# Weight parts side by side in one tile, and the feed-forward pool 32 bytes lower, in a float32 decoder trunk on one Trainium2 core

## Chip, core and metric

The kernel runs on one NeuronCore of a Trainium2 chip. The metric is the device time of one execution in microseconds (us). SBUF is the on-chip memory of 128 partitions from which every operand of the matrix engine is read; a tile's address is a byte offset that is the same in all its partitions.

## What is computed

Two layers on 512 tokens of width 1024, float32. Each layer is a half-step SwiGLU feed-forward block, a mixer, and a second half-step feed-forward block; the mixer is causal pooling in layer 0 and multi-head latent attention (MLA) in layer 1.

```python
def swiglu(h, w_gate, w_up, w_down):
    return (jax.nn.silu(h @ w_gate) * (h @ w_up)) @ w_down

for i in range(DEPTH):
    h = rmsnorm(x, ffn1_norm[i])
    x = x + FFN_HALF * swiglu(h, ffn1_w_gate[i], ffn1_w_up[i], ffn1_w_down[i])
    h = rmsnorm(x, mix_norm[i])
    x = x + (pool_mixer(h, ...) if i % 2 == 0 else mla_mixer(h, ...))
    h = rmsnorm(x, ffn2_norm[i])
    x = x + FFN_HALF * swiglu(h, ffn2_w_gate[i], ffn2_w_up[i], ffn2_w_down[i])
```

The widths are 1024 for the model and 2816 (22 blocks of 128) for the feed-forward layer.

## The kernel before

**Split products.** Every float32 operand is split into a high part and a low part (`split`, L113 to L122): ScalarE (ACT) writes the high part, VectorE (DVE) the difference. A product is then three matmuls per block of 128 rows (`mm3`, L107): high weights by high data, high weights by low data, low weights by high data. The weights are the stationary operand, which is loaded before each matmul (row kind PEld, LDWEIGHTS); the data are the moving operand, 256 or 512 columns of a `slot` tile.

**Weights.** SyncE's queue loads each block of 128 by 1024 weights into a tile `raw`, and `split` turns it into `whi` and `wlo`. The pool `wp` has three buffers each of `raw`, `whi` and `wlo`. `weights` (L124) makes a `whi` or `wlo` tile of 32 float32 more than is needed, so that `off` can start the data 64 bytes into it: `load_w` (L129) uses offset 0 in the feed-forward and most MLA products, 64 in `latent` (L702). The three buffers of a tag are taken in turn.

**A feed-forward block** works through the 22 blocks of its hidden width in chunks of 4, 6, 6, 6. The first chunk uses plain products of 512 columns. In the other three, `Two` (L367) computes two hidden blocks by two halves of the model width and two halves of the tokens with seven products instead of eight: each product is 4 row blocks of 3 matmuls with 256 columns. `w_sums` (L336) prepares its weights. Four of the seven products have their weights in `whi`/`wlo` at offset 64: a11, a12 from `raw`, and s1, s2 from a sum tile `s`. Three (s3, s4 and a22) have them in tiles `hi`/`lo` of the pool `fp`, which lives as long as the feed-forward block. Six `Two` make one chunk, 504 matmuls; there are 12 such chunks and so 72 `Two`. After each chunk the down projection makes 8 tiles of weights by `load_w` at offset 0, with 3 matmuls of 512 columns for each hidden block of the chunk, 18 in the later chunks, and adds the result to the stream `xs`.

**Pools.** SBUF pools lie behind one another in the order `cp`, `xp`, `sp` (45 `slot` tiles), `wp`, `kp`, `tp`, and then, one at a time, `fp` (feed-forward), `rp` (tables), `pp` (pooling) or `mp` (MLA). The order of the instructions on an engine follows the code, up to small shifts that a scheduler makes.

**The shared rotary key** of MLA (L726) takes a `whi` tile alone, without a `wlo`, and puts both parts into it. From then on `whi` is one buffer ahead of `wlo` in its turn.

Of the kernel before, what the change touches and what calls it, by code (L numbers as in the profile page):

```python
# [10 lines left out]
F32R = mybir.dt.float32r  # L11
# [6 lines left out]
P = 128  # L18
# [4 lines left out]
NT = S // P  # L23
# [8 lines left out]
WC = 1024  # L32
# [44 lines left out]
def trunk(ctx: ExitStack, tc: tile.TileContext, a: dict, out: bass.AP):  # L77
# [5 lines left out]
    wp = ctx.enter_context(tc.tile_pool(name="wp", bufs=3))  # L83
# [8 lines left out]
    def aux():  # L92
        return pb.tile([P, S], F32, tag="aux", name="aux")
# [7 lines left out]
    def small(n, dt=F32, tag=None, bufs=3):  # L101
        return tp.tile([P, n], dt, tag=tag or f"sm{n}", name="small", bufs=bufs)

    def mm(ps, lhsT, rhs, start, stop, skip=False):
        nc.tensor.matmul(ps, lhsT, rhs, start=start, stop=stop, skip_group_check=skip)  # L105
# [7 lines left out]
    def split(src, hi, lo, scale=None):  # L113

        if scale is None:
            nc.scalar.activation(hi, src, AF.Copy)  # L116
            nc.vector.tensor_tensor(out=lo, in0=src, in1=hi.bitcast(F32), op=ALU.subtract)  # L117
        else:
            nc.scalar.activation(hi, src, AF.Copy, scale=scale)  # L119
            nc.vector.scalar_tensor_tensor(  # L120
                out=lo, in0=src, scalar=scale, in1=hi.bitcast(F32), op0=ALU.mult, op1=ALU.subtract
            )  # L122

    def weights(tag, off=0):  # L124

        t = wp.tile([P, WC + 32], F32R, tag=tag, name=tag)
        return t[:, off // 4 : off // 4 + WC]

    def load_w(src, cols, off=0):  # L129
        raw = wp.tile([P, WC], F32, tag="raw", name="raw")  # L130
        hi, lo = weights("whi", off), weights("wlo", off)
        nc.sync.dma_start(raw[:, :cols], src)
        split(raw[:, :cols], hi[:, :cols], lo[:, :cols])
        return hi, lo
# [12 lines left out]
    def rsqrt(v, n, out=None):  # L147
        i = small(n, I32, tag=f"rsi{n}")
        nc.vector.tensor_scalar(i, v.bitcast(I32), 1, None, op0=ALU.logical_shift_right)
        y = small(n, tag=f"rsy{n}")  # L150
        nc.vector.tensor_scalar(
            y.bitcast(I32), i, -1.0, float(0x5F3759DF), op0=ALU.mult, op1=ALU.add
        )
        for last in (False, False, True):
            t = small(n, tag=f"rst{n}")
            nc.vector.tensor_mul(t, y, y)
            nc.vector.scalar_tensor_tensor(
                out=t, in0=t, scalar=-0.5, in1=v, op0=ALU.mult, op1=ALU.mult
            )
            y2 = out if last and out is not None else small(n, tag=f"rsy{n}")  # L160
            nc.vector.scalar_tensor_tensor(
                out=y2, in0=t, scalar=1.5, in1=y, op0=ALU.add, op1=ALU.mult
            )
            y = y2
        return y


    class Prep:
# [31 lines left out]
        def rstd(self):  # L200

            ps = aux()
            for i in range(NT):
                mm(ps[:, i : i + 1], self.sq[:, i * P : (i + 1) * P], ones[:, 0:1], True, True)
            v = small(NT, tag="ms")
            nc.vector.tensor_scalar(v, ps[:, :NT], 1.0 / D, EPS, op0=ALU.mult, op1=ALU.add)
            return rsqrt(v, NT, tp.tile([P, NT], F32, tag="rstd", name="rstd", bufs=2))

# [11 lines left out]
    def opening(wg, wu, prep):  # L220

        half = WC // 2
        ws = []
        for _ in range(2):
            raw = wp.tile([P, WC], F32, tag="raw", name="raw")
            ws.append((raw, weights("whi"), weights("wlo")))

        def load_half(e):
            for w, (raw, _, _) in zip((wg, wu), ws):
                nc.sync.dma_start(  # L230
                    raw[:, e * half : (e + 1) * half], w[:, e * half : (e + 1) * half]
                )

        def split_half(e):
            hs = slice(e * half, (e + 1) * half)
            for raw, hi, lo in ws:
                split(raw[:, hs], hi[:, hs], lo[:, hs])

        def load_x(j):
            nc.sync.dma_start(xs[j], a["xT"][j])  # L240

        load_x(0)
        load_half(0)
        for j in range(1, 4):
            load_x(j)
        load_half(1)
        for j in range(4, KD):
            load_x(j)
        nc.sync.dma_start(ident, a["ident"])
        ps = [acc(), acc()]  # L250
        for k in range(KD):
            prep.halve(k)
            if k % 4 == 0:
                split_half(k // 4)
            ks = slice(k * P, (k + 1) * P)
            for p, (_, hi, lo) in zip(ps, ws):
                mm3(p, (hi[:, ks], lo[:, ks]), prep.halves[k], k == 0, k == KD - 1)
        for k in (*range(1, KD), 0):
            prep.square(k)
        return ps  # L260
# [6 lines left out]
    def ffn_in(fp, wg, wu, wd, prep, nxt, first, final):  # L267
# [68 lines left out]
        def w_sums(top, low):  # L336

            hw = WC // 2
            rt = wp.tile([P, WC], F32, tag="raw", name="raw")
            rl = wp.tile([P, WC], F32, tag="raw", name="raw")  # L340
            nc.sync.dma_start(rt, top)
            nc.sync.dma_start(rl, low)
            a11, a12, a21, a22 = rt[:, :hw], rt[:, hw:], rl[:, :hw], rl[:, hw:]
            s12 = fp.tile([P, WC], F32, tag="s", name="s", bufs=2)
            s34 = fp.tile([P, WC], F32, tag="s", name="s", bufs=2)
            s1, s2, s3, s4 = s12[:, :hw], s12[:, hw:], s34[:, :hw], s34[:, hw:]
            for out, x, y, op in (
                (s1, a21, a22, ALU.add), (s2, s1, a11, ALU.subtract),
                (s3, a11, a21, ALU.subtract), (s4, a12, s2, ALU.subtract),
            ):  # L350
                nc.vector.tensor_tensor(out=out, in0=x, in1=y, op=op)  # L351

            def halves(src, n, tag):
                if tag == "w":
                    hi, lo = weights("whi", 64), weights("wlo", 64)
                else:
                    hi, lo = (
                        fp.tile([P, n], F32R, tag=tag + e, name=e, bufs=2) for e in ("hi", "lo")
                    )
                split(src, hi, lo)  # L360
                return [(hi[:, c : c + hw], lo[:, c : c + hw]) for c in range(0, n, hw)]

            a11, a12 = halves(rt, WC, "w")
            s3, s4 = halves(s34, WC, "c")
            s1, s2 = halves(s12, WC, "w")
            (a22,) = halves(a22, hw, "d")
            return a11, a12, a22, s1, s2, s3, s4  # L367
# [90 lines left out]
        for f0, f1 in CHUNKS:  # L458
# [38 lines left out]
            for m in range(KD):  # L497
                if f0 == 0 and m % 2 and m > 1:
                    x_sums(m // 2)
                hi, lo = load_w(wd[m][:, f0 * P : f1 * P], nf * P)  # L500
# [183 lines left out]
    def mla_layer(prep, nxt):  # L684
        with tc.tile_pool(name="mp", bufs=1) as mp:
# [16 lines left out]

            def latent(m):

                hi, lo = load_w(a["w_in"][m], WC, 64)
                p = acc()
                for k in range(KD):
                    ks = slice(k * P, (k + 1) * P)
                    mm3(p, (hi[:, ks], lo[:, ks]), xh[k], k == 0, k == KD - 1)
                lat[m] = (slot(), slot())  # L710
                split(p, *lat[m], gains[:, G_Q + m : G_Q + m + 1])
                e = m // KQ
                if e not in sums:
                    sums[e] = kp.tile([P, S], F32, tag="rows", name="lsq", bufs=2)
                    nc.scalar.activation(sums[e], p, AF.Square)
                else:
                    q = work()
                    nc.scalar.activation(q, p, AF.Square)
                    nc.vector.tensor_add(sums[e], sums[e], q)
# [4 lines left out]


            raw = wp.tile([P, WC], F32, tag="raw", name="raw")  # L726
            both = weights("whi")
            nc.sync.dma_start(raw[:, : KD * DR], a["w_kpe"])
            wv = both.rearrange("p (k e f) -> p k e f", k=KD, e=2)
            split(  # L730
# [49 lines left out]
            def latent_rms(e, n):  # L780

                ps = aux()
                for i in range(NT):
                    mm(ps[:, i : i + 1], sums[e][:, i * P : (i + 1) * P], ones[:, 0:1], True, True)
                v = small(NT, tag="ms")
                nc.vector.scalar_tensor_tensor(
                    out=v, in0=ps[:, :NT], scalar=1.0 / n, in1=r2, op0=ALU.mult, op1=ALU.mult
                )
                nc.vector.tensor_scalar(v, v, EPS, None, op0=ALU.add)
                f, f2 = keep(NT, f"f{e}"), keep(NT, f"ff{e}")  # L790
                nc.vector.tensor_mul(f, rsqrt(v, NT), r)
                nc.vector.tensor_mul(f2, f, f)
                return f, f2
# [389 lines left out]
```

## Time and profile before

| what | value |
|---|---|
| median of 3 runs | 1646.99 us (1646.85 to 1647.1) |
| the profiled execution's own time | 1648.0 us |
| its span in the trace | 1646.2 us |
| PE (matmul) busy | 1635.4 us, 99% of the span |
| PEld (weight loads) busy | 1476.7 us, 90% |
| DVE busy | 1250.8 us, 76% |
| ACT busy | 823.7 us, 50% |
| POOL (GpSimd) busy | 47.1 us, 3% |
| DMA | 161.74 MB, mean 98 GB/s |

Matmuls are pipelined: a row's duration reaches from a matmul's start to its modelled end, and the next has long begun by then. What a matmul costs in a dense stretch is therefore the distance between two starts, which the view of instructions in order of time gives, and not the mean duration of a group.

### The profile page before, as it was taken

The numbers are of one execution on the slowest core, as the hardware profiler recorded it, in microseconds if no ns is written. First come the engines' busy times: TensorE is split into PE (matmuls) and PEld (weight loads), VectorE is DVE, ScalarE is ACT, GpSimd is POOL, SyncE is SP. The second block draws the span as 40 slices with busy tenths as digits, with TensorE's granted clock in tenths as the row PEclk, the third lists the DMA queues.
The fourth block names the chain that finished last, engine by engine and source line by source line (L and its number), as shares of the span: only waits on it lengthen the run. The fifth ranks groups of instructions, "written<-read, shape, count | busy, mean of one in ns | idle before, by whom it ended". The sixth has DMA issues, their size and how long they took to land.

```text
span 1646.2 us, 26418 instructions
## 1 busy us (share of the span) xinstructions
PE 1635.4 (99%) x10502; PEld 1476.7 (90%) x10502; DVE 1250.8 (76%) x2114; ACT 823.7 (50%) x1409; POOL 47.1 (3%) x133
## 2 busy tenths in 40 slices
PE   8999999999999999999999999999999999999999
PEld 6898999988898989988999989888898889999897
DVE  8985858799986758669858667647788899677673
ACT  6453535554553535434635445447675455445351
POOL 0000000000000000000000000002321000000000
PEclk9999999999999999999999999999999999999999
DMA  5333324231333233332323243322122224333432
GB/s 169 103 111 114 107 82 127 84 114 58 119 107 110 93 106 103 96 103 84 125 85 124 81 125 93 95 93 62 46 59 77 73 62 136 90 116 97 118 94 90
DMA packets 52827, 161.74 MB, mean 98 GB/s; under 512 B 6240, under 2 KB 7008, under 8 KB 52704
## 3 DMA queue, kind: packets, MB, share of 16 engines
q1 hardware_dynamic: 52128, 159.34, 31.7%
q8 instruction: 82, 1.34, 0.3%
q10 hardware_dynamic: 576, 0.72, 0.1%
q14 instruction: 41, 0.34, 0.1%
HBM read 157.94 MB, written 2.10 MB: 97 GB/s over the span
## 4 chain that ended last, share of the span: by engine, by line
PE 96%; DVE 2%; ACT 1%; DMA 1%; issue 0%; SPq 0%; POOL 0%; DVEq 0%; POOLq 0%
PE acc L105 94%; PE aux L697 1%; PE aux L105 1%; PE aux L978 0%; DVE wlo L117 0%; DMA raw<-in_ffn_up 0%; DMA raw<-in_ffn_gate 0%; DVE s L351 0%; DVE slot L117 0%; ACT slot L119 0%; DVE x L510 0%; ACT whi L116 0%; ACT work L184 0%; DVE sqacc L185 0%; ACT work L959 0%
## 5 line engine op out<-in xcount | busy, mean ns | idle before, releaser
L105 PE MATMUL acc<-slot,whi 128*128 128x256 f32 (+1 forms) x4508 | 1091.2, 334 | 5.5 <-ACT whi L116 5.1
L105 PEld LDWEIGHTS acc<-slot,whi 128*128 128x128 f32 x4508 | 763.1, 189 | 102.2 <-ACT whi L116 5.1
L105 PE MATMUL acc<-slot,wlo 128*128 128x512 f32 (+1 forms) x2246 | 751.3, 335 | 0.2 <-DVE wlo L117 0.2
L105 PEld LDWEIGHTS acc<-slot,wlo 128*128 128x128 f32 x2246 | 422.2, 188 | 45.2 <-DVE wlo L117 0.9
L116 ACT ACTIVATE whi<-raw 128x1024 fp32r<-128x1024 f32 (+2 forms) x269 | 246.0, 915 | 378.9 <-PE acc L105 262.5
L117 DVE TENSOR_TENSOR wlo<-raw,whi 128x1024 fp32r<-128x1024 f32 (+2 forms) x268 | 278.9, 1042 | 105.1 <-ACT whi L116 103.5
L105 PE MATMUL acc<-slot,hi 128*128 128x256 f32 x1728 | 308.8, 279 | 0.0
L105 PEld LDWEIGHTS acc<-slot,hi 128*128 128x128 f32 x1728 | 263.3, 188 | 0.0
L105 PE MATMUL acc<-slot,lo 128*128 128x256 f32 x864 | 240.7, 279 | 0.0
L510 DVE SCALAR_TENSOR_TENSOR x<-acc,x 128x512 f32<-128x512 f32 x129 | 88.2, 684 | 134.5 <-PE acc L105 134.4
L105 PEld LDWEIGHTS acc<-slot,lo 128*128 128x128 f32 x864 | 162.4, 188 | 0.0
L398 ACT ACTIVATE m<-acc 128x256 f32<-128x256 f32 x216 | 81.9, 380 | 96.5 <-PE acc L105 95.9
L117 DVE TENSOR_TENSOR lo<-s,hi 128x1024 fp32r<-128x1024 f32 x72 | 88.0, 1222 | 55.1 <-ACT hi L116 53.5
L351 DVE TENSOR_TENSOR s<-raw 128x512 f32<-128x512 f32 x144 | 96.1, 685 | 19.3 <-DMA raw<-in_ffn_up 14.9
L116 ACT ACTIVATE hi<-s 128x1024 fp32r<-128x1024 f32 x72 | 76.2, 1058 | 45.6 <-PE acc L105 41.7
L105 PE MATMUL acc<-whi,slot 128*128 128x384 f32 (+2 forms) x320 | 87.8, 343 | 0.0
L117 DVE TENSOR_TENSOR wlo<-s,whi 128x1024 fp32r<-128x1024 f32 x72 | 87.7, 1217 | 0.0
L116 ACT ACTIVATE whi<-s 128x1024 fp32r<-128x1024 f32 x72 | 76.0, 1056 | 18.2 <-PE acc L105 12.9
L441 DVE TENSOR_TENSOR z<-acc,m 128x256 f32<-128x256 f32 (+1 forms) x144 | 79.2, 550 | 6.8 <-PE acc L105 6.4
L116 ACT ACTIVATE hi<-raw 128x512 fp32r<-128x512 f32 x72 | 45.6, 634 | 68.2 <-PE acc L105 42.5
L116 ACT ACTIVATE slot<-z 128x512 fp32r<-128x512 f32 x72 | 43.7, 623 | 37.3 <-DVE z L434 36.9
L105 PEld LDWEIGHTS acc<-whi,slot 128*128 128x128 f32 x320 | 56.9, 188 | 2.6 <-ACT whi L116 0.3
(176 smaller groups left out, 1306.5 us busy)
## 6 DMA issues: line engine op xcount, KB each, us to landing
raw<-in_ffn_gate SPq DMA_DIRECT2D x87, 512.0 KB, 3.5
raw<-in_ffn_up SPq DMA_DIRECT2D x87, 512.0 KB, 3.6
raw<-in_ffn_down SPq DMA_DIRECT2D x96, 384.0 KB, 3.2
raw<-in_ffn_down SPq DMA_DIRECT2D x32, 256.0 KB, 2.7
raw<-in_w_q SPq DMA_DIRECT2D x12, 384.0 KB, 3.1
raw<-in_w_in SPq DMA_DIRECT2D x8, 512.0 KB, 3.5
raw<-in_w_out SPq DMA_DIRECT2D x8, 512.0 KB, 3.5
x<-in_xT SPq DMA_DIRECT2D x8, 256.0 KB, 5.7
```

What stands on the lines that cost most here:

```text
L105: nc.tensor.matmul(ps, lhsT, rhs, start=start, stop=stop, skip_group_check=skip)
L116: nc.scalar.activation(hi, src, AF.Copy)
L117: nc.vector.tensor_tensor(out=lo, in0=src, in1=hi.bitcast(F32), op=ALU.subtract)
L351: nc.vector.tensor_tensor(out=out, in0=x, in1=y, op=op)
L398: nc.scalar.activation(self.kept[:, c[(1, 6, 7).index(n)]], part, AF.Copy)
L441: nc.vector.tensor_tensor(out=out, in0=x, in1=y, op=ALU.add)
L510: nc.vector.scalar_tensor_tensor(out=xs[m][:, cs], in0=p[:, cs], scalar=0.5, in1=xs[m][:, cs], op0=ALU.mult, op1=ALU.add,)
L697: nc.tensor.transpose(p[:, i * P : (i + 1) * P], src(i), ident)
```

## The change

A high and a low part now lie in one tile `wsp` of 2 x 1024 + 64 float32, 8448 bytes, the low part directly behind the high part; `off` moves both. `latent` uses offset 0 in place of 64. The small tile `ms` has two buffers in place of three, which makes the pool `tp` 32 bytes shorter, so that whatever comes after it (`fp`, `rp`, `pp`, `mp`) starts 32 bytes lower. The rotary key takes a whole `wsp` and uses half of it.

```diff
-    def weights(tag, off=0):
-        t = wp.tile([P, WC + 32], F32R, tag=tag, name=tag)
-        return t[:, off // 4 : off // 4 + WC]
+    def weights(off=0):
+        t = wp.tile([P, 2 * WC + 64], F32R, tag="wsp", name="wsp")
+        o = off // 4
+        return t[:, o : o + WC], t[:, o + WC : o + 2 * WC]
 
     def load_w(src, cols, off=0):
         raw = wp.tile([P, WC], F32, tag="raw", name="raw")
-        hi, lo = weights("whi", off), weights("wlo", off)
+        hi, lo = weights(off)
...
-            v = small(NT, tag="ms")
+            v = small(NT, tag="ms", bufs=2)
...
-            ws.append((raw, weights("whi"), weights("wlo")))
+            ws.append((raw, *weights()))
...
-                    hi, lo = weights("whi", 64), weights("wlo", 64)
+                    hi, lo = weights(64)
...
-                hi, lo = load_w(a["w_in"][m], WC, 64)
+                hi, lo = load_w(a["w_in"][m], WC)
...
-            both = weights("whi")
+            both = weights()[0]
```

Where the tiles start, in bytes within a partition, in the two built programs, with the remainder on division by 256 in brackets:

```
                      before                               changed
slot (45)             22944 + 2048 n  [160]                the same
whi, buffers 0 1 2    127392 [160] 131616 [32] 135840 [160]  (wsp) 127392 [160] 135840 [160] 144288 [160]
wlo, buffers 0 1 2    140064 [32]  144288 [160] 148512 [32]  wsp + 4096 [160]
the same, offset 64   [224] [96] [224] and [96] [224] [96]   all [224]
fp: hi                184192, 188288, 208768, 210816 [128]   each 32 lower [96]
fp: lo                200576, 204672, 212864, 214912 [128]   each 32 lower [96]
mp: vhi, vlo          198240, 202336, 206432, 210528 [96]    each 32 lower [64]
```

A block of 128 float32 columns is 512 bytes, so every block of a weight tile and every half of a `slot` keeps its tile's remainder.

The instructions of each engine are the same in kind and number. Their order shifts in a few places. On DVE in the first chunk of the first feed-forward block (L283/L296 gate and up values, L316 and L329 normalised halves and their sums, L117 low parts), before:

```order
L329 TENSOR_TENSOR m<-s,m 128x256
L316 SCALAR_TENSOR_TENSOR clo<-x_84,gains,rows 128x512
L117 TENSOR_TENSOR slot<-work,slot 128x512 [waits Activation_49]
L316 SCALAR_TENSOR_TENSOR clo<-x_88,gains,rows 128x512
L117 TENSOR_TENSOR slot<-m,slot 128x512 [waits Activation_49]
L117 TENSOR_TENSOR wlo<-raw,whi 128x512 [waits DMAHW4_49]
L117 TENSOR_TENSOR slot<-m,slot 128x512 [waits Activation_49]
L283 TENSOR_TENSOR work<-acc,rows 128x512 [waits PE_49]
L117 TENSOR_TENSOR slot<-clo,slot 128x512 [waits Activation_49]
```

and now (line numbers are one higher from L126 on):

```order
L330 TENSOR_TENSOR m<-s,m 128x256 [waits DVE_49]
L117 TENSOR_TENSOR slot<-work,slot 128x512 [waits Activation_49]
L317 SCALAR_TENSOR_TENSOR clo<-x_84,gains,rows 128x512
L117 TENSOR_TENSOR slot<-m,slot 128x512 [waits Activation_49]
L317 SCALAR_TENSOR_TENSOR clo<-x_88,gains,rows 128x512
L117 TENSOR_TENSOR slot<-m,slot 128x512 [waits Activation_49]
L284 TENSOR_TENSOR work<-acc,rows 128x512 [waits PE_49]
L117 TENSOR_TENSOR slot<-clo,slot 128x512 [waits Activation_49]
L117 TENSOR_TENSOR wsp<-raw,wsp 128x512 [waits DMAHW4_49]
```

The low part of the first down-projection weights moves three places back; the same work stands around it.

On PE at the start of the pooling layer (`maps` are the matmuls with `whi` or `wsp` as moving operand; the four of one column are the sum of squares of `rstd`), before:

```order
L105 MATMUL acc_3816<-whi_3759,slot_3477 128x256
L105 MATMUL acc_3816<-whi_3759,slot_3509 128x256
L105 MATMUL acc_3816<-wlo_3760,slot_3509 128x256
L105 MATMUL aux_3790<-ones_90,sqacc_3448 128x1 x4
L105 MATMUL acc_3816<-whi_3759,slot_3510 128x256
```

and now:

```order
L105 MATMUL acc_3700<-wsp_3683,slot_3471 128x256
L105 MATMUL acc_3739<-wsp_3683,slot_3375 128x256
L105 MATMUL aux_3713<-ones_90,sqacc_3379 128x1 x4
L105 MATMUL acc_3739<-wsp_3683,slot_3375 128x256
L105 MATMUL acc_3739<-wsp_3683,slot_3376 128x256
```

The four matmuls of `rstd` come seven `maps` matmuls earlier, behind 25 of them instead of 32.

## Rows read from the trace of the kernel before

**Rows 1.** The page: busy time by engine, and the chain that ended last.
```profile
PE 1635.4 (99%) x10502; PEld 1476.7 (90%) x10502; DVE 1250.8 (76%) x2114; ACT 823.7 (50%) x1409; POOL 47.1 (3%) x133
...
PE 96%; DVE 2%; ACT 1%; DMA 1%; issue 0%; SPq 0%; POOL 0%; DVEq 0%; POOLq 0%
```

**Rows 2.** Waits of PE: engine line waited for: us in total, times, longest us.
```profile
PE acc L105 <- ACT whi L116: 5.1, 1, 5.1
```

**Rows 3.** Groups by shape: matmuls in 0 to 1072.4 us, 1072.4 us to the end, whole span.
```profile
L105 PE MATMUL acc<-slot,whi 128*128 128x512 f32 x1472 | 462.9, 395 | 5.3 <-ACT whi L116 5.1 <-DVE slot L120 0.2
L105 PE MATMUL acc<-slot,wlo 128*128 128x512 f32 x736 | 293.1, 398 | 0.0
...
L105 PE MATMUL acc<-slot,whi 128*128 128x512 f32 x709 | 220.9, 394 | 0.0
L105 PE MATMUL acc<-slot,wlo 128*128 128x512 f32 x347 | 136.9, 395 | 0.0
...
L105 PE MATMUL acc<-slot,hi 128*128 128x256 f32 x1728 | 308.8, 279 | 0.0
L105 PE MATMUL acc<-slot,lo 128*128 128x256 f32 x864 | 240.7, 279 | 0.0
...
L105 PE MATMUL acc<-whi,slot 128*128 128x384 f32 x192 | 54.1, 344 | 0.0
L105 PE MATMUL acc<-slot,vhi 128*128 128x256 f32 x96 | 20.0, 289 | 0.6 <-ACT slot L116 0.6
L105 PE MATMUL acc<-slot,vlo 128*128 128x256 f32 x48 | 13.3, 278 | 0.0
```

**Rows 4.** PE in order of time (start us, us, instruction), a layer-0 down projection: both ends.
```profile
226.74 0.63 PE L105 MATMUL acc<-slot,whi 128*128 128x512 f32 x2
...
260.13 0.40 PE L105 MATMUL acc<-slot,whi 128*128 128x256 f32 x2
```

**Rows 5.** PE in order of time, a down projection of the last block: starts of tiles.
```profile
1518.17 0.62 PE L105 MATMUL acc<-slot,whi 128*128 128x512 f32 x2
...
1522.34 0.62 PE L105 MATMUL acc<-slot,whi 128*128 128x512 f32 x2
...
1526.42 0.62 PE L105 MATMUL acc<-slot,whi 128*128 128x512 f32 x2
...
1534.77 0.62 PE L105 MATMUL acc<-slot,whi 128*128 128x512 f32 x2
...
1538.88 0.62 PE L105 MATMUL acc<-slot,whi 128*128 128x512 f32 x2
...
1551.34 0.40 PE L105 MATMUL acc<-slot,whi 128*128 128x256 f32 x2
```

**Rows 6.** PE in order of time, the rotary key's matmuls and the one behind them.
```profile
1072.48 4.04 PE L105 MATMUL acc<-slot,whi 128*128 128x512 f32 x17
```

**Rows 7.** PE in order of time, within the first chunk of `Two`s: starts of products.
```profile
184.02 0.39 PE L105 MATMUL acc<-slot,whi 128*128 128x256 f32 x2
...
185.38 0.39 PE L105 MATMUL acc<-slot,whi 128*128 128x256 f32 x2
...
186.74 0.40 PE L105 MATMUL acc<-slot,hi 128*128 128x256 f32 x2
...
188.14 0.40 PE L105 MATMUL acc<-slot,hi 128*128 128x256 f32 x2
...
189.54 0.39 PE L105 MATMUL acc<-slot,whi 128*128 128x256 f32 x2
```

**Rows 8.** ACT and DVE in order of time, the split of s1 and s2 there.
```profile
184.16 1.06 ACT L116 ACTIVATE whi<-s 128x1024 fp32r<-128x1024 f32 x1
...
185.71 1.22 DVE L117 TENSOR_TENSOR wlo<-s,whi 128x1024 fp32r<-128x1024 f32 x1
```

**Rows 9.** Stretches: bounds, length, busy us (count) of PE, PEld, DVE, ACT, POOL; clock, DMA.
```profile
168.50:226.70 58.20, 58.18 (x505) 57.97 (x504) 44.36 (x61) 32.43 (x50) 0.00 (x0) 1.00 0.32 95
26.90:76.80 49.90, 49.90 (x217) 40.62 (x217) 47.74 (x81) 26.12 (x40) 0.00 (x0) 1.00 0.26 75
```

More of the change, by code (lines that the diff above doesn't have):

```diff
@@ L784, in latent_rms @@
                     mm(ps[:, i : i + 1], sums[e][:, i * P : (i + 1) * P], ones[:, 0:1], True, True)
-                v = small(NT, tag="ms")
+                v = small(NT, tag="ms", bufs=2)
                 nc.vector.scalar_tensor_tensor(
```

## The prediction

> **What bounds the kernel.** First I read the page's busy times and its chain: PE is busy for 99% of the span, and the chain that ended last runs over PE for 96% of it [rows 1]. Then the waits of PE: the longest is 5.1 us, once, on the first weights of all [rows 2]. So nothing that feeds PE is late, and a change can only move the end by changing what a matmul costs on PE itself, or by making something late that is not so now. What a matmul costs is read as the distance between the starts of matmuls in the view in order of time. The change leaves every instruction in place but for the small shifts shown, and alters addresses. So the question is whether that distance hangs on addresses, and it does.
>
> **Matmuls of 512 columns.** In the down projections the moving operand is always a `slot`, remainder 160 on division by 256. Before the rotary key the pairs (`whi`, `wlo`) have remainders (160, 32), (32, 160), (160, 32) in turn: one of the two is always off by 128 from the moving operand. Eight tiles of 18 matmuls take 260.13 - 226.74 = 33.39 us, 231.9 ns a matmul [rows 4]. The rotary key takes a `whi` alone, and from then on the pairs are (160, 32), (32, 32) and (160, 160). That is an experiment that the old kernel makes by itself. In the last block (32, 32) takes 1522.34 - 1518.17 = 4.17 us for 18 matmuls, 231.7 ns; (160, 160) takes 1526.42 - 1522.34 = 4.08 us, 226.7 ns; the next (160, 160) takes 1538.88 - 1534.77 = 4.11 us, 228.3 ns [rows 5]. All eight tiles there take 1551.34 - 1518.17 = 33.17 us, 230.3 ns [rows 5], less than in layer 0, since a third of the tiles has become shorter. So equal remainders of high and low part are not enough, as (32, 32) shows; both must have that of the moving operand. The rotary key itself reads 16 blocks from a `whi` of remainder 160 only: 17 matmuls take 4.04 us, of which the last one's own duration of some 0.395 us [rows 3] goes off, so 16 distances take 3.64 us, 227.8 ns [rows 6].
>
> After the change all three tiles have remainder 160 in both parts at offset 0, so every weight of these products is of the good kind. I take 227.8 ns for all, the mean of 226.7, 228.3 and a second 228.3 that I assume for the third such tile, which is also the rotary key's value. The count is 1472 + 736 = 2208 matmuls up to the rotary key and 709 + 347 = 1056 from it on [rows 3]. They come to 2208 x (231.9 - 227.8) = 9.1 us and 1056 x (230.3 - 227.8) = 2.6 us: **11.7 us less**. The bounds are the two measured tiles: 226.7 ns gives 2208 x 5.2 + 1056 x 3.6 = 15.3 us, 228.3 ns gives 2208 x 3.6 + 1056 x 2.0 = 10.1 us. `latent`, which goes from offset 64 to 0, is counted with the rest.
>
> **Matmuls of 256 columns in `Two`.** Here the best place is another one. Products with weights in `whi`/`wlo` at offset 64 (remainders 224 and 96, which is 64 away from the 160 of the `slot`s on either side) take 186.74 - 185.38 = 1.36 us, and the one before it 185.38 - 184.02 = 1.36 us. Products with weights in `hi`/`lo` (remainder 128, 32 away) take 188.14 - 186.74 = 1.40 us and 189.54 - 188.14 = 1.40 us [rows 7]. Both remainders go with one speed, so what counts is the distance of 64. With the pool 32 bytes lower `hi`/`lo` come to 96, which is one of the two good remainders. The gain is 0.04 us, with starts given to 0.01 us anything from 0.03 to 0.05 us, for each of 72 x 3 = 216 products (1728 + 864 = 2592 matmuls [rows 3], 12 in each): 6.5 to 10.8 us. I take 0.035 us, the lower half, since the 42 products of a whole chunk take 58.20 us [rows 9], 1.386 us on average, and 24 at 1.36 with 18 at 1.40 would be 57.84: even a product of the 1.36 us kind now and then takes longer, and that the change leaves. **7.5 us less.** The `whi`/`wlo` products stay on their level: at offset 64 all weights have 224 now, where two of three `whi` had it before.
>
> **What else moves.** The pool of MLA starts 32 bytes lower too; `vhi` and `vlo` (96 and 48 matmuls as weights [rows 3]) go from remainder 96 to 64. I expect the difference between the two kinds of products there, 0.04 us / 12 = 3 ns a matmul: 144 x 3 = 0.5 us more; the bound below is nothing, the bound above 1 us. Where `whi` and `wlo` are the moving operand (pooling, and 192 matmuls of 384 columns as the largest group [rows 3]), the `slot`s are the weights and the same remainders meet; no row parts the cases, so I take nothing, with 1 us on either side. The earlier `rstd` in the pooling layer and the shifted low part on DVE move work within stretches that PE does not wait in; nothing, 0.5 us on either side. Fewer `ms` buffers cost nothing: that tile is read a few instructions after it is written, and the next is a whole stage later or, in MLA, has the second buffer.
>
> A new tile is free only when the low part's last matmul has been read too, so ACT's split of the high part begins one matmul later, by 0.11 us in a `Two` (1.36 us / 12) and 0.23 us in a down projection. What covers it: the split of s1 and s2 starts on ACT at 184.16 us, its low part ends on DVE at 185.71 + 1.22 = 186.93 us [rows 8], and the product that needs it starts at 189.54 us [rows 7]. 2.6 us are to spare, so 0.11 us costs nothing. The DVE queue behind it waits as little. If PE gets faster, DVE and ACT have to keep up: in a chunk of `Two`s DVE is busy for 44.36 of 58.20 us, in the first chunk of a block for 47.74 of 49.90 us [rows 9]. That last one is tight, but those 217 matmuls get only 217 x 4.1 ns = 0.9 us shorter, and 2.2 us are free.
>
> **Sum.** 1648.0 (the profiled execution) - 11.7 - 7.5 + 0.5 = 1629.3 us. The median of the runs shown is 1.0 us lower than that execution, so **1628 us** in its terms. With every bound on the good side (15.3, 10.8, and 2 of the rest) it is 1619, with every bound on the bad side (10.1, 6.5, less 2.5) 1633.
>
> **Rivals.**
> *Only the pool shift acts* (the (160, 160) tiles owe their time to something else of the last block): 1647 - 7 = 1640 us. Against it: (32, 32) and (160, 160) alternate there within 4 us, in the same stage [rows 5].
> *Only the common tile acts* (96 is no good for `hi`/`lo`): 1647 - 11.7 + 0.5 = 1636 us. For it: the products of 1.40 us differ from those of 1.36 us in their pool as well as in their remainder. Against: nothing else about them differs on PE [rows 7].
> *Nothing*: PE's costs do not hang on addresses. The differences of rows 5 and 7 would be chance, and the time 1647 us. The rows repeat too well for that. [...] The trace disagrees, with 1.40 against 1.36 us for the same product.
> *Slower: the weights come late.* High and low part now fall free together. If the split of s1 and s2 in each `Two` slips by more than its 2.6 us, through the longer wait and the queue behind it on ACT and DVE, PE waits in every `Two`: 72 us for each microsecond beyond. From 19/72 = 0.26 us beyond on the gain is gone; at 0.35 us the time is 1628 + 25 = 1653 us. For it: DVE at 96% in the first chunk. Against: the slip to be expected is 0.11 us.
>
> **How the numbers follow.** The forecast has 0.78, the pool shift alone 0.06, the common tile alone 0.08, nothing 0.04, late weights 0.04. The range of 1619 to 1637 us takes in the forecast's bounds and the common tile alone. Faster by over 0.2% (3.3 us, about what a measurement can tell from no change): 0.78 + 0.06 + 0.08 = 0.92; within 0.2%: 0.04; slower: 0.04.
>
> **What would show it.** In the changed profile a tile of 18 matmuls in any down projection should take 4.08 to 4.11 us, in every buffer, where now one buffer pair in three takes that after the rotary key and none before it; eight tiles 32.8 us in place of 33.39. All seven products of a `Two` should take 1.36 us, and a chunk of `Two`s some 57.6 us. PE's waits should stay as short as they are. If tiles stay at 4.17 us the first term is wrong, if `hi` products stay at 1.40 the second; a wait of PE on ACT or DVE in the `Two`s would speak for the last rival.

## The result, and the profile after

The changed kernel takes 1628.3 us (median of 4 runs, 1627.84 to 1630.2) against 1647.05 us for the kernel before on the same chip: a ratio of 0.9889, 95% interval 0.9873 to 0.9904, 18.7 us less. The forecast was 1628 us. The profiled execution took 1628.72 us with a span of 1626.8 us, 19.4 us shorter than before.

The page of the changed kernel, busy times and the chain, beside [rows 1]:

```profile
PE 1615.0 (99%) x10502; PEld 1465.8 (90%) x10502; DVE 1250.0 (77%) x2114; ACT 821.9 (51%) x1409; POOL 48.3 (3%) x133
...
PE 91%; DVE 3%; DMA 2%; ACT 2%; issue 1%; SPq 0%; POOL 0%; ACTq 0%; DVEq 0%; POOLq 0%
```

PE does the same 10502 matmuls and is still busy for 99% of the span, but 20.4 us less. DVE and ACT are as they were.

PE in order of time, the down projection of layer 0 that answers to [rows 4], and the one of the last block that answers to [rows 5] (one name now covers both parts, so consecutive matmuls merge into one row):

```profile
223.20 33.06 PE L105 MATMUL acc<-slot,wsp 128*128 128x512 f32 x146
...
1500.34 33.06 PE L105 MATMUL acc<-slot,wsp 128*128 128x512 f32 x146
```

The last two of the 146 are already of 256 columns, so the 144 take 33.06 - 0.28 (the last one's own duration) - 0.11 (one distance) = 32.67 us, 226.9 ns each, in both places. They took 33.39 and 33.17 us before. The difference between the early and the late part of the kernel is gone, as every pair of parts is now at remainder 160.

PE in order of time, starts of products in the second chunk of `Two`s (165.6 to 223.2 us), the same chunk that [rows 7] are from (their heading says the first, but 184 us lies in the second, which begins at 168.5 us there):

```profile
168.44 0.40 PE L105 MATMUL acc<-slot,hi 128*128 128x256 f32 x2
...
169.85 4.56 PE L105 MATMUL acc<-slot,wsp 128*128 128x256 f32 x36
...
175.60 0.39 PE L105 MATMUL acc<-slot,hi 128*128 128x256 f32 x2
...
176.96 1.52 PE L105 MATMUL acc<-slot,wsp 128*128 128x256 f32 x12
...
178.32 0.39 PE L105 MATMUL acc<-slot,hi 128*128 128x256 f32 x2
...
179.68 4.24 PE L105 MATMUL acc<-slot,wsp 128*128 128x256 f32 x36
```

From 175.60 on every product takes 1.36 us, whichever pool its weights are in. The first `hi` product of the chunk, 169.85 - 168.44 = 1.41 us, does not; that becomes important below. The stretch of this chunk, and PE's waits:

```profile
165.60:223.20 57.60, 57.58 (x505) 57.37 (x504) 44.40 (x61) 32.47 (x50) 0.00 (x0) 1.00 0.31 95
```

```profile
PE acc L105 <- ACT wsp L116: 5.1, 1, 5.1
PE acc L105 <- DVE lo L117: 0.9, 1, 0.9
```

57.60 us where 58.20 stood [rows 9], and one wait of 0.9 us that was not there.

Over the whole trace I added up the distances from each matmul's start to the next one's, by kind of weight:

| matmuls | before | after | difference | forecast |
|---|---|---|---|---|
| 3262 of 512 columns, weights `whi`/`wlo` or `wsp` | 761.4 us | 747.2 us | -14.2 | -11.7 |
| 2592 of 256 columns, `hi`/`lo` | 301.8 us | 295.7 us | -6.1 | -7.5 |
| 3491 of 256 columns, `whi`/`wlo` or `wsp` | 401.8 us | 402.4 us | +0.6 | 0 |
| 144 with `vhi`/`vlo` | 18.14 us | 18.46 us | +0.3 | +0.5 |
| 1012 others | 154.6 us | 154.5 us | -0.1 | 0 |

They come to -19.5 us, against 19.4 us of span.

### The profile page after: what moved, and what is told of

The parts are those of the page before. It is cut to its first block, busy times and chain, and to the rows that moved or that the text cites. A ratio compares the mean times of both kernels' runs of the same rounds, so it can differ in the third digit from the quotient of the medians.

```text
span 1626.8 us, 26356 instructions
## 1 busy us (share of the span) xinstructions
PE 1615.0 (99%) x10502; PEld 1465.8 (90%) x10502; DVE 1250.0 (77%) x2114; ACT 821.9 (51%) x1409; POOL 48.3 (3%) x133
## 4 chain that ended last, share of the span: by engine, by line
PE 91%; DVE 3%; DMA 2%; ACT 2%; issue 1%; SPq 0%; POOL 0%; ACTq 0%; DVEq 0%; POOLq 0%
PE acc L105 89%; DMA raw<-in_ffn_up 1%; DMA raw<-in_ffn_gate 1%; DVE s L352 1%; DVE wsp L117 1%; PE aux L698 1%; PE aux L105 1%; ACT wsp L116 1%; PE aux L979 0%; DVE x L511 0%; ACT work L960 0%; ACT slot L116 0%; DVE slot L117 0%; ACT work L848 0%; ACT slot L119 0%
## 5 line engine op out<-in xcount | busy, mean ns | idle before, releaser
L105 PE MATMUL acc<-slot,wsp 128*128 128x256 f32 (+1 forms) x6754 | 1177.8, 332 | 6.2 <-ACT wsp L116 5.1
L105 PEld LDWEIGHTS acc<-slot,wsp 128*128 128x128 f32 x6754 | 1019.8, 188 | 138.1 <-ACT wsp L116 5.1
L116 ACT ACTIVATE wsp<-raw 128x1024 fp32r<-128x1024 f32 (+2 forms) x269 | 246.1, 916 | 358.5 <-PE acc L105 230.5
L117 DVE TENSOR_TENSOR wsp<-raw,wsp 128x1024 fp32r<-128x1024 f32 (+2 forms) x269 | 280.1, 1042 | 103.2 <-ACT wsp L116 101.5
L117 DVE TENSOR_TENSOR lo<-s,hi 128x1024 fp32r<-128x1024 f32 x72 | 88.0, 1223 | 50.7 <-ACT hi L116 50.6
L399 ACT ACTIVATE m<-acc 128x256 f32<-128x256 f32 x216 | 81.4, 379 | 82.2 <-PE acc L105 80.4
L105 PE MATMUL acc<-wsp,slot 128*128 128x384 f32 (+2 forms) x480 | 94.7, 342 | 0.1
L117 DVE TENSOR_TENSOR wsp<-s,wsp 128x1024 fp32r<-128x1024 f32 x72 | 87.8, 1219 | 0.0
L116 ACT ACTIVATE wsp<-s 128x1024 fp32r<-128x1024 f32 x72 | 76.2, 1059 | 20.6 <-PE acc L105 13.6
L105 PEld LDWEIGHTS acc<-wsp,slot 128*128 128x128 f32 x480 | 78.6, 189 | 4.8 <-DVE wsp L117 0.8
L117 DVE TENSOR_TENSOR slot<-z,slot 128x512 fp32r<-128x512 f32 x72 | 48.4, 686 | 8.4 <-ACT slot L116 8.4
L430 ACT ACTIVATE z<-z 128x768 f32<-128x768 f32 x36 | 30.6, 849 | 37.1 <-DVE z L442 37.0
```

What stands on the lines that cost most here:

```text
L399: nc.scalar.activation(self.kept[:, c[(1, 6, 7).index(n)]], part, AF.Copy)
L430: nc.scalar.activation(two.z[:, C:], two.z[:, C:], AF.Silu)
```

## The experiments

Theory: the distance between two matmuls hangs on where their weights lie relative to the moving operand, by the remainder of the address on division by 256, and the two parts of the change act each by itself. Rivals: the parts work only together; the joining of two tiles into one acts (one release, fewer waits), not the address. Every run has the changed kernel's order of instructions on every engine, but for the pool shift alone, which has the order of the kernel before. So among all the others only addresses and the number of small `ms` buffers differ. (Between the two orders the traces show roughly a hundred of DVE's 2114 instructions and some twenty of ACT's 1409 in another place, more than the example given with the change.) Five runs are single executions; what is read from them are the distances in their traces, at a granted clock of 1.00 as everywhere here.

**The common tile alone.**

```diff
-            v = small(NT, tag="ms", bufs=2)
+            v = small(NT, tag="ms")
```

> The common weight tile alone: the changed kernel with three ms buffers again, so that every pool behind them, the feed-forward one among them, lies where it did (hi/lo at remainder 128), and the same order of instructions as the changed kernel. Theory (each address acts by itself): tiles of 18 matmuls of 512 columns stay at 4.08 us; hi/lo products are back at 1.40 us, 216 x 0.03 = 6.5 us, and vhi/vlo give back 0.6 us: 1628.3 + 6 = 1634 us. Rival (the two parts only work together): 1647 us. Rival (the pool shift does nothing): 1628 us.

Measured: 1636.9 us, ratio to before 0.9939 (0.9922 to 0.9955).

**The pool shift alone**, in the kernel before.

```diff
-            v = small(NT, tag="ms")
+            v = small(NT, tag="ms", bufs=2)
```

> The pool shift alone: the kernel before with two ms buffers, order of instructions as before. Theory: hi/lo products at 1.36 us, all else as before, vhi/vlo 0.6 us dearer: 1647 - 6 = 1641 us, and with the run of the common tile alone the two gains add up to that of the change. Rival (only together): 1647 us. Rival (the shift does nothing): 1647 us with hi/lo products still at 1.40 us.

Measured: 1639.8 us, ratio 0.9954 (0.9939 to 0.9969). The `hi` matmuls by group, first with the common tile alone, then with the pool shift alone, where [rows 3] have 308.8 us and 279 ns:

```profile
L105 PE MATMUL acc<-slot,hi 128*128 128x256 f32 x1728 | 309.0, 279 | 0.0
```

```profile
L105 PE MATMUL acc<-slot,hi 128*128 128x256 f32 x1728 | 301.2, 276 | 0.0
```

10.6 and 7.7 us below the 1647.5 us of before: together 18.3 us, the gain of the change. The parts add up; "only together" falls. The common tile alone was 3 us slower than I expected: the distances of its 512-column matmuls sum to 747.8 us, as in the change, but its `Two`s take 705.9 against 698.1 us, 7.8 where I had allowed 6.5.

**The low part 128 bytes further on in the same tile.**

```diff
-        return t[:, o : o + WC], t[:, o + WC : o + 2 * WC]
+        return t[:, o : o + WC], t[:, o + WC + 32 : o + 2 * WC + 32]
```

> The changed kernel with the low part 128 bytes further into the same common tile: high at remainder 160, low at 32; tiles, buffers, waits and order of instructions as in the changed kernel. Theory (the address acts, not the joining into one tile): 18 matmuls of 512 columns at 4.16 us again, 231.5 against 227.0 ns, 3262 x 4.5 ns = 14.7 us more: 1643 us; products of Two unchanged, since 96 is as good there as 224. Rival (one tile, one release, fewer waits made it faster): 1628 us.

Measured: 1638.84 us, ratio 0.9947 (0.9933 to 0.9962), 10.5 us above the change. PE in order of time, the same down projection with the 24 matmuls of 256 columns behind it, with the low part off and in the changed kernel:

```profile
224.93 36.22 PE L105 MATMUL acc<-slot,wsp 128*128 128x512 f32 x168
```

```profile
223.20 35.66 PE L105 MATMUL acc<-slot,wsp 128*128 128x512 f32 x168
```

0.56 us for one projection. Over the kernel the matmuls of 512 columns sum to 760.2 us, 13.0 more than in the change, though tiles, releases and order are the same: the address acts, and the joining falls as the cause of this term. The total is 4 us below the expectation: 1.7 us of it since I had put 4.5 ns on each matmul, where 4.0 were measured, and 2.8 us since the `Two`s got shorter (695.3 against 698.1 us), which I had not expected.

**512 columns at offset 64.**

```diff
-        hi, lo = weights(off)
+        hi, lo = weights(off or 64)
```

> The changed kernel with every load of 512-column weights at offset 64: remainder 224 in both parts, the place that is best for 256 columns. Theory (512 columns want remainder 160): 231.5 to 233 ns against 227.0, 3214 x 5.5 ns = 18 us more: 1646 us. Rival (only that high and low agree with each other counts): 1628 us.

Measured: 1644.22 us (one run). The same stretch as above:

```profile
225.74 36.48 PE L105 MATMUL acc<-slot,wsp 128*128 128x512 f32 x168
```

The matmuls of 512 columns sum to 767.0 us, 19.8 more. High and low agree with each other here; it does not help. Of the places tried for 512 columns (both parts at 160, 747.2 us; the low one at 32, 760.2 us; both at 224, 767.0 us) the remainder of the moving operand, 160, is the best. Again the `Two`s got shorter, by 3.9 us.

**`Two` at offset 0.**

```diff
-                    hi, lo = weights(64)
+                    hi, lo = weights()
```

> The changed kernel with the whi/wlo weights of Two at offset 0 in place of 64 bytes: remainder 160, that of the slots. Theory (for 256 columns the best place is another one than for 512): 120 against 113.8 ns a matmul, as in the few products of MLA at that remainder, so 3456 x 6.2 ns = 21 us more: 1649 us, hi/lo products unchanged. Rival (the remainder of the moving operand is good for every matmul): 1628 us or less.

Measured: 1648.14 us, ratio 1.0005 (0.9996 to 1.0015). PE in order of time, one `wsp` product in the same chunk, where the changed kernel has 1.52 us:

```profile
180.02 1.60 PE L105 MATMUL acc<-slot,wsp 128*128 128x256 f32 x12
```

The `wsp` matmuls of 256 columns sum to 423.3 us, 20.9 more; `hi`/`lo` stay at 295.4 us. Of the places tried, the best for 512 columns is the worst for 256: 423.3 us / 3491 = 121.3 ns a matmul, against 115.3 in the changed kernel. As expected, to 1 us.

**`hi`/`lo` at 160.**

```diff
-            v = small(NT, tag="ms", bufs=2)
+            v = small(NT, tag="ms", bufs=4)
```

> The changed kernel with four ms buffers: the feed-forward pool 64 bytes higher, hi/lo at remainder 160, that of the slots; MLA's vhi/vlo at 128. Theory (the distance to the moving operand counts, 0 is worse than 32): 120 against 113.6 ns, 2592 x 6.4 ns = 17 us more: 1645 us. Rival (any move away from 128 helps hi/lo): 1628 us.

Measured: 1657.67 us (one run), 12.7 us above the expectation. A `wsp` product, and the `hi` group:

```profile
180.17 1.58 PE L105 MATMUL acc<-slot,wsp 128*128 128x256 f32 x12
```

```profile
L105 PE MATMUL acc<-slot,hi 128*128 128x256 f32 x1728 | 317.3, 283 | 0.0
```

`hi`/`lo` sum to 310.8 us, 15.1 more, near the 17 expected. But the `wsp` products, at the address they have in the changed kernel, sum to 415.7 us, 13.3 more. The theory that a matmul's cost hangs on its own addresses alone is not enough. Four more runs went after that.

**`hi`/`lo` at 160, and `wsp` of `Two` at 96.**

```diff
-                    hi, lo = weights(64)
+                    hi, lo = weights(192)
...
-            v = small(NT, tag="ms", bufs=2)
+            v = small(NT, tag="ms", bufs=4)
```

> As the run with hi/lo at 160, but the whi/wlo weights of Two at offset 192 bytes: remainder 96 in place of 224. In that run the whi/wlo products of Two took 1.41 us although their own address had not changed. Theory (matmuls of 256 columns keep the pace that the products before them left, and weights at 96 restore it where weights at 224 do not, as in the run with Two at 0, where products at 96 follow products at 160 and take 1.36 us): the whi/wlo products are back at 1.36 us, 1657.7 - 13 = 1645 us. Rival (the other users of the feed-forward pool, ACT and DVE on s, m and z at remainder 160, hold PE up): 1.41 us stays, 1657 us.

Measured: 1646.0 us (one run). The `wsp` product is back:

```profile
178.89 1.52 PE L105 MATMUL acc<-slot,wsp 128*128 128x256 f32 x12
```

`wsp` sums to 403.1 us, `hi`/`lo` to 312.0. ACT and DVE use the same pool at the same place as in the run before, so they are not what held PE up.

**`Two` at offset 0, and `hi`/`lo` at 224.**

```diff
-                    hi, lo = weights(64)
+                    hi, lo = weights()
...
-            v = small(NT, tag="ms", bufs=2)
+            v = small(NT, tag="ms", bufs=6)
```

> The run with the whi/wlo of Two at remainder 160, with hi/lo at 224 in place of 96. Theory (weights at 224 keep the pace that products at 160 left): the hi/lo products take 1.41 us in place of 1.36, 216 x 0.05 = 11 us more than that run: 1659 us. Rival (a product's pace hangs on its own addresses alone): 1.36 us, 1648 us.

Measured: 1659.59 us (one run). `hi`/`lo` sum to 306.8 us, 11.4 more than behind the same `wsp` products with `hi`/`lo` at 96. As expected: behind products at 160, products at 224 took 118.4 ns a matmul on the mean (306.8 us / 2592), and products at 96 took 114.0 (295.4 us / 2592).

**`hi`/`lo` at 224, `wsp` unchanged.**

```diff
-            v = small(NT, tag="ms", bufs=2)
+            v = small(NT, tag="ms", bufs=6)
```

> The changed kernel with six ms buffers: hi/lo at remainder 224, 64 away from the slots on the other side, where the whi/wlo of Two are already; MLA's vhi/vlo at 192. Theory (a distance of 64 on either side): all products of Two at 1.36 us, 1628.5 us, vhi matmuls at 120 ns. Rival (96 alone is good, 224 only lives on its neighbours): hi/lo products at 1.40 us or more, 1635 us or more.

Measured: 1642.06 us (one run): the expectation falls. PE in order of time, a `wsp` product in the first chunk of `Two`s and one in the second:

```profile
87.23 1.52 PE L105 MATMUL acc<-slot,wsp 128*128 128x256 f32 x12
...
177.71 1.58 PE L105 MATMUL acc<-slot,wsp 128*128 128x256 f32 x12
```

All `Two` weights are at 224 here. Seven of the twelve chunks run at 117.8 ns a matmul from end to end, five change to 113.3 ns within their first six products, and none changes back. Each of the five changes stands right behind a pause of PE; the last section comes back to that.

**`wsp` of `Two` at 96 like `hi`/`lo`**, a try at a better kernel.

```diff
-                    hi, lo = weights(64)
+                    hi, lo = weights(192)
```

> The changed kernel with the whi/wlo weights of Two at offset 192 bytes, remainder 96, like hi/lo: a try at a better kernel. Theory (96 holds the pace better than 224): 113.4 in place of 113.8 ns on 6048 matmuls, 2.4 us: 1626 us. Rival (both sides alike): 1628.5 us.

Measured: 1652.66 us, ratio 1.003 (1.0018 to 1.0041), 24 us above the changed kernel where 2 us less were expected: the expectation falls. All weights of `Two` are at 96, and all twelve chunks run at 117.8 ns a matmul:

```profile
179.69 1.57 PE L105 MATMUL acc<-slot,wsp 128*128 128x256 f32 x12
```

```profile
L105 PE MATMUL acc<-slot,hi 128*128 128x256 f32 x1728 | 311.6, 279 | 0.0
```

**MLA's pool back by 32 bytes**, and the changed kernel on the same chip.

```diff
+            mp.tile([P, 8], F32, name="pad")
             mask = mp.tile([P, P], F32, name="mask")
```

> The changed kernel with 32 bytes of padding at the head of MLA's pool, so that vhi/vlo are back at remainder 96 while the feed-forward pool stays lowered. Theory: 144 matmuls get 3 to 4.5 ns cheaper, 0.5 us: 1627.7 us, no difference that the clock on the whole kernel can show, but the mean distance of the vhi matmuls back from 120 to 116 ns. Rival (vhi does not hang on its address): 120 ns stays.

> The changed kernel itself, on the same chip as the padded MLA pool, to compare the two: 1628.3 us, with PE waiting 0.9 us once for a low part (hi/lo of the first Two behind a first chunk) as in its first profile, if that wait belongs to the order of the instructions and not to that one execution.

Measured: 1629.46 us (1628.08 to 1630.22) and 1628.77 us (1628.18 to 1629.87), no difference that the time can show. The `vhi` matmuls, first padded, then not:

```profile
L105 PE MATMUL acc<-slot,vhi 128*128 128x256 f32 x96 | 20.0, 289 | 0.7 <-ACT slot L116 0.7
```

```profile
L105 PE MATMUL acc<-slot,vhi 128*128 128x256 f32 x96 | 20.5, 293 | 0.6 <-ACT slot L116 0.6
```

The 84 distances without a wait average 115.7 against 120.1 ns. The price was there and is 0.4 us, less than the spread of the runs. The wait on a low part was 0.5 us in this second profile of the changed kernel; it was absent with the padded pool, in the same order of instructions. So some executions have it and others do not.

## Why the prediction was right

**What bounds the kernel** held: the gain came out of the distances between matmuls, -19.5 of 19.4 us.

**The first term**, 512 columns at remainder 160, was right in its cause, the address, and 2.5 us too small: -14.2 for -11.7 us. The mis-sized term is the 227.8 ns, the mean of the two measured (160, 160) tiles and of a third that I assumed to be as long as the longer one. In the changed kernel a down projection runs at 226.9 ns. Between tiles of other remainders one (160, 160) tile took 226.7 ns a matmul and another 228.3 [rows 5]; among its own kind the mean of eight is 226.9. The low part 128 bytes off (13.0 us more) shows that it is the address, and offset 64 for 512 columns (19.8 us more) that equal remainders at another place do not do it.

**The second term**, `hi`/`lo` in the `Two`s, was right in sign and near in size, -6.1 for -7.5 us, but the reason given for it was only half of it. The step that failed is "both remainders go with one speed, so what counts is the distance of 64". [Rows 7] could not show that: before the rotary key the pairs at offset 64 are (224, 96), (96, 224), (224, 96), so each of the two products of 1.36 us had one part at 224 and the other at 96, and neither remainder was seen alone. In these runs weights 64 away from the moving operand went at 113.3 ns a matmul and also at 117.8: with everything at 224, seven of twelve chunks had 117.8 from end to end, and five went over to 113.3 and kept it. With every weight of the `Two`s at 96 the kernel takes 24 us more than the changed one, and with every one at 224 it takes 14 us more. The weights of the changed kernel go to and fro between 224 and 96, and that is the mix in which the short distance was seen. That the change kept such a mix, and did not put all weights on one remainder, was luck: the reasoning did not ask for it. The gain stopped short of 7.5 us mainly by the one wait for a low part: the two distances around it are 1.17 and 0.22 us in place of 0.12 each, some 1.2 us. The first `hi` or `lo` product of each chunk, still at the longer distance (1.41 us at 168.44), costs 12 x 0.05 = 0.6 us; the forecast had taken 0.035 and not 0.04 us a product for such things.

**The third**, that `vhi`/`vlo` get dearer by some 0.5 us, was right, 0.3 to 0.4 us.

**What was costed at nothing**: the later split of the high part cost nothing in the changed kernel, where PE waits for ACT's high parts of weights 5.1 us once, as before; 2.6 us were to spare by [rows 7] and [rows 8]. The shifted order on DVE was costed at nothing too. Behind the first chunk of the second feed-forward block PE waits up to 0.9 us once for a low part, 0.05% of the time. What makes that part late is not separated. In DVE's order another low part, which came after it, now comes before it; and the work that leads to it begins when a load of weights lands, here in the changed kernel and with the padded MLA pool, which has the same order and not this wait:

```profile
429.73 1.29 DVE L352 TENSOR_TENSOR s<-raw 128x512 f32<-128x512 f32 x2 [2.31 <-DMA raw<-in_ffn_gate]
```

```profile
428.73 1.29 DVE L352 TENSOR_TENSOR s<-raw 128x512 f32<-128x512 f32 x2 [1.40 <-DMA raw<-in_ffn_gate]
```

**The rivals.** Only one of the parts acting, and nothing: each falls with the two runs of one part alone. Were PE's costs free of addresses, all these times would be alike; runs that differ in nothing but addresses and the number of small `ms` buffers lie between 1628 and 1660 us. Late weights did not come: the one new wait is the 0.9 us above, where that rival has one in each of the 72 `Two`s.

## What to carry to other kernels

Where PE is busy throughout (99% of the span here), look at the distance between the starts of its matmuls tile by tile, and set it beside the address of each weight tile: a kernel whose buffers differ in remainder makes the experiment by itself. Test an address rule for one stage at a time, since of the places tried 512 columns were best with the weights at the moving operand's remainder (226.9 ns a matmul) and 256 columns worst (121.3 ns). And test it in the final mix: 96 was good for `hi`/`lo` beside `wsp` at 224 (295.7 us, where 128 took 301.8) and bad when all weights of the `Two`s had it (24 us more), so an address that was fitted by single rows is checked by a run that moves everything there.

## What the runs showed that was not expected

In these runs a stream of 256-column matmuls mostly kept its pace. With weights 64 away from the moving operand there were two, 113.3 and 117.8 ns a matmul. A chunk behind a down projection with all parts at 160 started at 117.8 ns. It went over to 113.3 ns where products at 224 and at 96 alternate (the changed kernel), and where products at 96 follow products at 160 (`Two` at offset 0; `hi`/`lo` at 160 with `wsp` at 96). It stayed at 117.8 ns in all twelve chunks with everything at 96, in seven of twelve with everything at 224, and near it, 118.4 ns on the mean, for `hi`/`lo` at 224 that follow products at 160, apart from single ones right behind a pause. Behind 512-column matmuls at 224 the `Two`s had 113.3 ns from the first product in ten of twelve chunks.

Where the weights' remainder did not change, the changes of pace stood behind a pause of PE, as all five did with everything at 224. In the fifth product of each chunk a weight load waits for ACT to copy out a partial sum (L399). The view of PE's waits hardly shows it, since a matmul's duration, 0.28 us, covers most of the gap (a distance of 0.30 us in eight of the changed kernel's twelve chunks, 0.36 in four). The weight loads' waits in the changed kernel:

```profile
PEld acc L105 <- ACT m L399: 2.9, 12, 0.3
```

There one distance of 0.28 us or more is followed by one of 219 to 227 ns. With the fifth product's weights at 224 (the changed kernel twice, the padded MLA pool, 512 columns at offset 64, and `hi`/`lo` at 224: 60 chunks), the stream went on at 113.3 ns where that second distance was 220 to 223 ns, and at 117.8 ns where it was 225 to 227 ns, whatever it had before; one chunk, with 219 ns and then 117.8, is the exception. So the changed kernel itself falls back to 117.8 ns there in two chunks of its first profile and in nine of its second, and returns to 113.3 ns a few products later, where a product at 224 follows one at 96. With everything at 96 all twelve chunks went on at 117.8 ns.

Why the pace is kept no run here settles. Nor is it shown that the weights' place relative to the moving operand counts, and not their own remainder: the `slot`s lie at 160 in every run. And one thing that the runs point to was not tried: the common tile with both parts at 160 for 512 columns, and in `Two` the low part at 96 with the high part at 224. In the run with the low part off, which had its `Two` weights so, every chunk reached 113.3 ns within its first product, and the `Two`s were 2.8 us shorter than in the changed kernel, of which some 1.2 us are the wait for a low part that this run did not have. So some 2 us may be left; this is an estimate and was not run.
